# Tiles of float32r operands placed at multiples of 128 bytes in their partition

## The chip, the core and the metric

The kernel runs on one core of a Trainium2 chip. The metric is the device time of one execution in microseconds, as a median over several runs. The work of the core is done by TensorE (PE for its matmuls, PEld for the loads of its stationary operand), VectorE (DVE), ScalarE (ACT), GpSimd (POOL) and the DMA queue of SyncE (SP).

## The reference

Two blocks of two layers each run one after the other on 256 rows of width 1,024, all in float32. The first is a conditioned mixer with attention, gated linear attention and convolution, over 256 rows of context and 256 rows of x, each layer followed by a gated feed-forward part:

```
def _ffn(h, p):
    return (jax.nn.silu(h @ p['w_ff_gate']) * (h @ p['w_ff_up'])) @ p['w_ff_down']
```

The second block has a mixer of three kinds of attention and a feed-forward part with a short convolution:

```
for l in range(DEPTH):
    h = rms_norm(x, attn_pre_norm[l])
    mix = hybrid_mixer(h, cos, sin, w_in[l], ..., w_out[l])
    x = x + rms_norm(mix, attn_post_norm[l])
    h = rms_norm(x, ffn_pre_norm[l])
    x = x + rms_norm(conv_ffn(h, w_up[l], conv_w[l], conv_b[l], w_down[l]), ffn_post_norm[l])
```

Nearly all arithmetic is in products of 256 rows with weight matrices: `w_in`, `w_out` and the three feed-forward matrices of each layer.

## The kernel before

A float32 product is made of three float32r products. `split` and `weights` cut each operand into a rounded part `hi` and a remainder `lo`, both float32r, and `mm3` (lines 218 to 222) adds hi·hi, hi·lo and lo·hi in PSUM. In `gemm_f` the weights are the stationary operand, 128 columns at a time, and 256 rows of the input stream through them (512 where two streams share a weight). In `gemm_t` the input is stationary, and up to 512 columns of the weights stream. In a profile's name such as `g<-b,hi` the moving operand stands first.

Weights come by DMA on SP's queue into `raw` (`load`), ACT copies them to `hi` (line 210), and DVE subtracts to `lo` (line 213). The order of instructions on each engine is the Tile framework's, from a simulated timeline and the priorities that the code sets (`later`, `slot`).

Tiles live in pools: `wts` (raw, hi, lo), `cst` (constants), `sml` (small statistics), `com` (the inputs' hi and lo, tag `b16`, and rows), then `first` for the first block, and inside it, in turn, `mix0`, `ff`, `mix1` and `fx`. In the second block, `sec0` takes the place of `first`. Pools and tiles lie one behind the other in each partition, after a scratch of 16 KB for DMA descriptors and four constants. `Core.tile` gives every tile of a pool the size that its shape has, rounded to 32 bytes.

The position of a float32r operand in its partition, taken modulo 128 bytes, is here called its remainder. In the built program `wts` begins at 16,512 (remainder 0) and its tiles are 4,096 bytes each. `cst` begins at 53,376 and holds two tiles `cb2` of 32 bytes each; through these, `com` begins at 61,248 (remainder 64). `first` begins at remainder 64, and a tile of 8 bytes in it, `one`, puts all that follows at 96. `mix0`, `mix1`, `ff` and `fx` lie at 96, and the operands of `sec0` at 32. The 14,136 float32r products of the program stand at these remainders:

| columns that stream | remainder of moving | remainder of stationary | products |
|---|---|---|---|
| 256 | 64 (`com`) | 0 (`wts`) | 8,320 |
| 256 | 64 (`com`, `first`) | 96 (`first`, `ff`, `mix0`, `mix1`) | 992 |
| 256 | 0 (`wts`) | 64 (`com`) | 368 |
| 256 | 96 | 64 | 80 |
| 512 | 0 (`wts`) | 64 (`com`) | 1,584 |
| 512 | 64 (`com`) | 0 (`wts`) | 912 |
| 512 | 0 (`wts`) | 96 (`ff`, `fx`) | 680 |
| 512 | 0 (`wts`) | 32 (`sec0`) | 456 |
| 512 | 32 or 96 | 64 (`com`) | 240 |
| 512 | 96 (`mix`, `ff`, `fx`) | 96 | 112 |
| 512 | 32 (`sec0`) | 32 (`sec0`) | 72 |
| 284, 192 or 2 | various | various | 320 |

The other matmuls of the program are transposes and products in float32 and a few in bfloat16; a product in plain float32 stands in the trace as two matmuls.

Of the kernel before, what the change touches and what calls it, by code (L numbers as in the profile page):

```python
# [9 lines left out]
F32 = mybir.dt.float32  # L10
F32R = mybir.dt.float32r
BF16 = mybir.dt.bfloat16
I32 = mybir.dt.int32
U8 = mybir.dt.uint8
# [11 lines left out]
def together(**groups):  # L26
# [22 lines left out]
    'pg': dict(g=4),  # L49
    'pt': dict(t=4),  # L50
}


class Layout:
# [111 lines left out]
class Core:  # L166
# [4 lines left out]
    def tile(self, pool, shape, dt=F32, tag=None, bufs=None):  # L171

        self.n += 1
        kind = pool.name.rstrip('0123456789')
        tag = SHARE.get(kind, {}).get(tag, tag)
        n = bufs or BUFS[kind].get(tag, 1)
        return pool.tile(list(shape), dt, name=f"{tag}_{self.n}", tag=tag, bufs=n)

    @contextmanager
    def later(self, n):  # L180
# [136 lines left out]
class Second(Core):  # L317
# [177 lines left out]
    def rope(self, pr, h0, n):  # L495
        nc = self.nc
        for t in range(2):
            x = pr[t][:, h0 * 64:(h0 + n) * 64].rearrange("p (h d) -> p h d", d=64)
            x1, x2 = x[:, :, 0:8], x[:, :, 8:16]
            cos = self.cs2[:, 0, t][:, None, :].to_broadcast([128, n, 8])  # L500
            sin = self.cs2[:, 1, t][:, None, :].to_broadcast([128, n, 8])
            a, b, c, d = [self.tile(self.P, [128, 14, 8], F32, 'rp')[:, :n] for _ in range(4)]
            nc.vector.tensor_mul(a, x1, cos)
            nc.vector.tensor_mul(b, x2, sin)
            nc.vector.tensor_mul(c, x2, cos)
            nc.vector.tensor_mul(d, x1, sin)
            nc.vector.tensor_sub(x1, a, b)
            nc.vector.tensor_add(x2, c, d)
# [203 lines left out]
    def attend(self, proj, pr, v, rb, src):  # L712

        nc = self.nc
        proj(5)

        ga = self.tile(self.P, [128, 2, 8, 3], F32, 'ga')
        lf, e, z = [self.tile(self.P, [128, 2, 4], F32, 'lf') for _ in range(3)]
        for t in range(2):
            nc.vector.tensor_add(z[:, t], pr[t][:, P2['ff']:P2['ff'] + 4], rb[:, 0:4])  # L720
            nc.vector.tensor_add(ga[:, t].rearrange("p h j -> p (h j)"), pr[t][:, P2['ng']:P2['ng'] + 24], rb[:, 4:28])
        nc.scalar.activation(ga, ga, AF.Tanh, scale=0.5)
        nc.vector.tensor_scalar(ga, ga, 0.5, 0.5, op0=ALU.mult, op1=ALU.add)
        nc.scalar.activation(e, z, AF.Abs)
        nc.scalar.activation(e, e, AF.Exp, scale=-1.0)
        nc.scalar.activation(e, e, AF.Ln, bias=1.0)
        nc.vector.scalar_tensor_tensor(lf, z, 0.0, e, op0=ALU.min, op1=ALU.subtract)
        proj(1)
        pc = self.tile(self.PT, [128, 512], F32, 't')[:4, :256]
        nc.tensor.matmul(pc[:, :128], lf[:, 0], self.c('tri'), start=True, stop=True)  # L730
        nc.tensor.matmul(pc[:, 128:], lf[:, 0], self.c('ones'), start=True, stop=False)
        nc.tensor.matmul(pc[:, 128:], lf[:, 1], self.c('tri'), start=False, stop=True)
        crow = self.tile(self.P, [128, 256], F32, 's1')[:4]
        nc.vector.tensor_scalar(crow, pc, -1.0, None, op0=ALU.mult)
        proj(2)


        qk = {}

        def heads(*which):  # L740
            ps = self.tile(self.PT, [128, 2, 256], F32, 't')
            for j, (n, i) in enumerate(which):
                col = P2[n] + 128 * i
                for t in range(2):
                    nc.tensor.transpose(ps[:, j, t * 128:t * 128 + 128], pr[t][:, col:col + 128], self.ident)
            o = self.tile(self.P, [128, 2, 256], F32, 'qk')
            f = 0.125 if which[0][0][1] == 'q' else 1.0
            if len(qk) % 4:
                nc.scalar.activation(o, ps, AF.Copy, scale=f)
            else:  # L750
                nc.vector.tensor_scalar(o, ps, f, None, op0=ALU.mult)
            for j, key in enumerate(which):
                qk[key] = o[:, j]
        self.rope(pr, 8, 14)
        heads(('dq', 0), ('dq', 1))
        heads(('dk', 0), ('dk', 1))
        heads(('ks', 0), ('kw', 0))
        hi, lo = self.pair()
        PT_, cmp, queue = {}, {}, []

        def units(*gens, depth=DEPTH):
            for u in gens:
                next(u)
                queue.append(u)
                while len(queue) > depth:
                    next(queue.pop(0), None)
        scores = lambda t, w: self.nsa_scores(t, w, ('ks', 'kw')[w], w + 1, pr, qk, ga, PT_)
        four = lambda kind, base, t: self.heads4(kind, base, t, pr, qk, crow, hi, lo)
        units(four('d', 0, 0), four('d', 0, 1))
        ck = self.compress('k', pr, v, src, cmp)  # L770
        next(ck)
        proj(0)
        self.rope(pr, 0, 8)
        heads(('nq', 0), ('nq', 1))
        heads(('nq', 2), ('nq', 3))
        units(scores(0, 0))
        proj(3)
        next(ck, None)
        units(scores(0, 1))
        heads(('fq', 0), ('fq', 1))  # L780
        heads(('fk', 0), ('fk', 1))
        proj(4)
        cv = self.compress('v', pr, v, src, cmp)
        next(cv)
        units(four('f', 2, 0))
        next(cv, None)
        units(four('f', 2, 1), scores(1, 0), self.nsa_compressed(0, qk, cmp, ga, PT_),
              self.nsa_out(0, pr, cmp, PT_, hi, lo), scores(1, 1), self.nsa_compressed(1, qk, cmp, ga, PT_),
              self.nsa_out(1, pr, cmp, PT_, hi, lo))
        units(depth=0)  # L790
        while queue:
            next(queue.pop(0), None)
        return hi, lo
# [88 lines left out]
class First(Core):  # L882
# [589 lines left out]
    def mixer(self, L, s, X, full=True, src=None, rope=None, hook=None, hT=None, late=None):  # L1472
# [5 lines left out]
        if late:  # L1478
            late[0]()
            late.pop()()  # L1480
        glu = lambda j: self.gemm_f2(L.src('glu', j), hX)
        tabs = self.tables(L, rope)
        if full:
            ys = []
# [202 lines left out]
def build(tc, I, out):  # L1687
    nc = tc.nc
    K = Kernel(tc)
    rows = lambda a: [a[t * 128:t * 128 + 128] for t in range(2)]  # L1690
    left = lambda ends: dict(enumerate(ends))
    with ExitStack() as es:
        pool = lambda e, name, space=None: e.enter_context(tc.tile_pool(name=name, bufs=1, **({'space': space} if space else {})))
# [15 lines left out]
        for l in range(2):  # L1709
            L = Layer1(l, I[f'w1{l}'], LAYOUT[0][l], I[f'row1{l}'])  # L1710
            L.a2 = I[f'a2{l}']
            L.vec = K.tile(K.C, [128, I[f'vec1{l}'].shape[1]], F32, 'vec1')
            nc.sync.dma_start(L.vec, I[f'vec1{l}'])
            L.cb2 = K.tile(K.C, [128, 8], F32, 'cb2')
            nc.vector.tensor_scalar(L.cb2, L.v('cb', 8), 2.0, None, op0=ALU.mult)
            Ls.append(L)
        with ExitStack() as e1:
# [4 lines left out]
            first = K.rest[:2]  # L1722
# [68 lines left out]
```

## Time and profile before

| | us |
|---|---|
| median of 3 runs | 2732.79 |
| lowest and highest run | 2726.75, 2738.06 |
| the profiled execution: its own time | 2729.63 |
| the profiled execution: span from first to last instruction | 2727.8 |
| TensorE busy with matmuls | 2621.6 |
| VectorE busy | 1954.7 |
| ScalarE busy | 1383.3 |
| GpSimd busy | 137.8 |

A busy time is the union of the spans of an engine's instructions. TensorE's matmuls overlap: a new one starts while the results of the one before still drain, so the duration of one (276 ns and more) is longer than the step from one start to the next (113 ns and more). This step is called the pace here. It is read from the starts in the timeline, or from the number of matmuls in a stretch in which PE never rests: the stretch and one duration together, divided by the number, since a matmul is counted that only reaches into the stretch.

### The profile page before, as it was taken

What the parts mean: (1) busy time and instruction counts of PE and PEld (TensorE: products, weight loads), DVE (VectorE), ACT (ScalarE), POOL (GpSimd) and SP (SyncE); (2) the same over time, 40 slices, a digit from 0 to 9 for tenths busy, and PEclk for the clock granted to TensorE, in tenths of its full rate; (3) what the DMA queues carried; (4) which work ended last, traced back from release to release, by engine and by line L of the source; (5) the groups of instructions that cost most, each with busy time, mean ns of one, the idle gap of its engine ahead of it and who ended that gap; (6) DMA issues with size and microseconds to landing.
All of it is one profiled execution on the core that took longest, in us unless ns stands there. A gap on an engine that the chain in (4) does not pass through costs nothing.

```text
span 2727.8 us, 45641 instructions
## 1 busy us (share of the span) xinstructions
PE 2621.6 (96%) x17408; PEld 2271.2 (83%) x17408; DVE 1954.7 (72%) x3942; ACT 1383.3 (51%) x2524; POOL 137.8 (5%) x280
## 2 busy tenths in 40 slices
PE   7999999999999999999999999989989999999999
PEld 5977999977989888887797898979976699776997
DVE  4988977899967633355688997666676689556895
ACT  3555555545555422234754654544454566544663
POOL 0010011000001100001100100010010000000000
PEclk8999999999999999999999999989999999999999
DMA  7566456565535422222455433545554355542454
GB/s 255 187 224 206 163 178 211 185 208 180 179 116 206 173 93 93 93 93 100 154 167 201 160 120 117 172 152 186 186 183 148 110 170 196 172 160 93 163 193 155
DMA packets 127915, 443.34 MB, mean 163 GB/s; under 512 B 14888, under 2 KB 19112, under 8 KB 127696
## 3 DMA queue, kind: packets, MB, share of 16 engines
q1 hardware_dynamic: 127696, 440.43, 47.8%
q8 instruction: 137, 2.24, 0.3%
q14 instruction: 82, 0.67, 0.1%
HBM read 435.09 MB, written 5.28 MB: 161 GB/s over the span
## 4 chain that ended last, share of the span: by engine, by line
PE 88%; DVE 3%; DMA 3%; ACT 3%; issue 1%; POOL 1%; SPq 0%; DVEq 0%; POOLq 0%; ACTq 0%
PE g L221 21%; PE g L220 21%; PE g L222 20%; PE t L220 3%; PE t L222 3%; PE t L221 3%; DMA raw<-in_w_dram 3%; PE g L925 2%; PE t L1175 1%; PE t L1149 1%; PE t L1277 1%; PE t L1262 1%; PE t L1112 1%; PE t L1184 1%; PE g L663 1%
## 5 line engine op out<-in xcount | busy, mean ns | idle before, releaser
L213 DVE TENSOR_TENSOR lo<-raw,hi 128x512 fp32r<-128x512 f32 (+2 forms) x1280 | 824.8, 684 | 358.0 <-issue 157.3
L210 ACT CAST hi<-raw 128x1024 fp32r<-128x1024 f32 (+2 forms) x644 | 672.4, 1046 | 731.3 <-PE g L221 256.6
L220 PE MATMUL g<-b,hi 128*128 128x256 f32 (+1 forms) x2912 | 833.5, 288 | 4.4 <-ACT hi L210 3.9
L221 PE MATMUL g<-b,hi 128*128 128x256 f32 (+1 forms) x2912 | 829.4, 286 | 2.6 <-DVE b L311 2.5
L222 PE MATMUL g<-b,lo 128*128 128x256 f32 (+1 forms) x2912 | 823.4, 288 | 1.1 <-DVE lo L213 1.1
L220 PEld LDWEIGHTS g<-b,hi 128*128 128x128 f32 x2912 | 548.9, 189 | 15.1 <-ACT hi L210 4.3
L221 PEld LDWEIGHTS g<-b,hi 128*128 128x128 f32 x2912 | 549.4, 189 | 12.0 <-DVE b L311 3.9
L222 PEld LDWEIGHTS g<-b,lo 128*128 128x128 f32 x2912 | 542.1, 188 | 10.3 <-DVE lo L213 1.9
L1289 DVE SCALAR_TENSOR_TENSOR yc<-yc,vec,yc 128x256 f32<-128x256 f32 x720 | 345.4, 480 | 10.8
L221 PE MATMUL g<-lo,b 128*128 128x512 f32 (+2 forms) x712 | 271.4, 382 | 2.0 <-DVE lo L213 2.0
L222 PE MATMUL g<-hi,b 128*128 128x512 f32 (+2 forms) x712 | 264.7, 372 | 0.5 <-DVE b L314 0.4
L220 PE MATMUL g<-hi,b 128*128 128x512 f32 (+2 forms) x712 | 254.1, 377 | 11.2 <-ACT hi L210 5.7
L220 PEld LDWEIGHTS g<-hi,b 128*128 128x128 f32 x712 | 133.8, 191 | 38.5 <-ACT hi L210 6.5
L221 PEld LDWEIGHTS g<-lo,b 128*128 128x128 f32 x712 | 135.7, 191 | 30.7 <-DVE lo L213 6.2
L222 PEld LDWEIGHTS g<-hi,b 128*128 128x128 f32 x712 | 135.5, 190 | 22.2 <-DVE b L314 1.1
L220 PE MATMUL t<-b,hi 128*128 128x256 f32 (+1 forms) x336 | 112.6, 335 | 0.0
L221 PE MATMUL t<-b,hi 128*128 128x256 f32 (+1 forms) x336 | 112.6, 335 | 0.0
L222 PE MATMUL t<-b,lo 128*128 128x256 f32 (+1 forms) x336 | 112.4, 335 | 0.0
L477 DVE SCALAR_TENSOR_TENSOR s<-g,vec,s 128x255 f32<-128x255 f32 (+1 forms) x176 | 84.0, 478 | 6.0 <-ACT s L475 3.9
L925 PE MATMUL g<-raw,cs 128*32 128x256 f32 x768 | 67.7, 432 | 19.0 <-DMA raw<-in_w_dram 18.8
L221 PEld LDWEIGHTS t<-b,hi 128*128 128x128 f32 x336 | 63.7, 190 | 7.3
L220 PEld LDWEIGHTS t<-b,hi 128*128 128x128 f32 x336 | 63.2, 188 | 7.4
(421 smaller groups left out, 3928.7 us busy)
## 6 DMA issues: line engine op xcount, KB each, us to landing
raw<-in_w_dram SPq DMA_DIRECT2D x772, 512.0 KB, 3.8
b<-in_row_dram SPq DMA_DIRECT2D x16, 512.0 KB
b<-in_ctx_dram SPq DMA_DIRECT2D x4, 512.0 KB
ends<-st SPq DMA_DIRECT2D x8, 256.0 KB
st<-ends SPq DMA_DIRECT2D x8, 256.0 KB
b<-in_x_dram SPq DMA_DIRECT2D x4, 512.0 KB, 5.5
b<-ctx SPq DMA_DIRECT2D x4, 512.0 KB
raw<-in_w_dram SPq DMA_DIRECT2D x4, 426.0 KB
```

Of the source, the lines that this page charges most:

```text
L210: self.nc.scalar.copy(hi[:, :m], p)
L213: self.nc.vector.tensor_sub(lo[:, q], p[:, q], hi[:, q].bitcast(F32))
L220: t.matmul(ps, a[0], b[0], start=first, stop=False)
L221: t.matmul(ps, a[0], b[1], start=False, stop=False)
L222: t.matmul(ps, a[1], b[0], start=False, stop=last)
L477: nc.vector.scalar_tensor_tensor(c[:, m, j:], ps[:, m, :256 - j], cw[:, ft, 2 - j:3 - j], c[:, m, j:], op0=ALU.mult, op1=ALU.add)
L663: nc.tensor.matmul(ps[:, b], qk['nq', a * per + b][s, t * 128:t * 128 + 128], qk[kn, 0][s, :nk], start=False, stop=b == per - 1)
L925: m = nc.tensor.matmul(ps[32 * q:32 * q + 32, n * 256:n * 256 + 256], self.cs[:, h * 4 + q], raw[:, q * 256:q * 256 + 256], start=h == 0, ...
L1112: nc.tensor.matmul(p[:, h], kw[:, d, h * 128:h * 128 + 128], vg[:, h * 256:h * 256 + 256], start=True, stop=True)
L1149: nc.tensor.matmul(o, w, self.U[d][:, b * 256:b * 256 + n], start=d + i == 0, stop=d + i == 2)
L1175: nc.tensor.matmul(ps[:, a, h], G[h][b][:, a] if b < 3 else kT[:, h, ts], G[h][b][:, 2 + a], start=True, stop=True)
L1289: e.scalar_tensor_tensor(o, y[:, j:j + 256], w[:, j:j + 1], o, op0=ALU.mult, op1=ALU.add)
```

## The change

Every tile of two dimensions in the pools `first`, `mix0`, `mix1`, `ff`, `fx` and `sec0` is allocated with its row rounded up to 128 bytes, and used in its old size. Four kinds of small tiles with more dimensions are written as two-dimensional ones, so that they fall under this. The two tiles `cb2` in `cst` become 64 bytes long instead of 32, which moves `sml` and `com` behind them by 64 bytes. The scratch for DMA descriptors shrinks from 16,384 to 4,096 bytes, which moves everything down by 12,288 bytes (96 times 128).

```diff
+ALIGN = 128
+ALIGNED = ('first', 'mix', 'ff', 'fx', 'sec')
...
         n = bufs or BUFS[kind].get(tag, 1)
-        return pool.tile(list(shape), dt, name=f"{tag}_{self.n}", tag=tag, bufs=n)
+        make = lambda s: pool.tile(s, dt, name=f"{tag}_{self.n}", tag=tag, bufs=n)
+        size = {F32: 4, F32R: 4, I32: 4, BF16: 2, U8: 1}[dt]
+        if kind in ALIGNED and len(shape) == 2 and shape[1] * size % ALIGN:
+            step = ALIGN // size
+            return make([shape[0], -(-shape[1] // step) * step])[:, :shape[1]]
+        return make(list(shape))
...
-            a, b, c, d = [self.tile(self.P, [128, 14, 8], F32, 'rp')[:, :n] for _ in range(4)]
+            a, b, c, d = [self.tile(self.P, [128, 112], F32, 'rp').rearrange("p (h n) -> p h n", n=8)[:, :n] for _ in range(4)]
...
-        ga = self.tile(self.P, [128, 2, 8, 3], F32, 'ga')
-        lf, e, z = [self.tile(self.P, [128, 2, 4], F32, 'lf') for _ in range(3)]
+        ga = self.tile(self.P, [128, 48], F32, 'ga').rearrange("p (t h n) -> p t h n", h=8, n=3)
+        lf, e, z = [self.tile(self.P, [128, 8], F32, 'lf').rearrange("p (t h) -> p t h", h=4) for _ in range(3)]
...
-            L.cb2 = K.tile(K.C, [128, 8], F32, 'cb2')
+            L.cb2 = K.tile(K.C, [128, 16], F32, 'cb2')[:, :8]
...
-    nc = bacc.Bacc("TRN2", target_bir_lowering=False, num_devices=1)
+    nc = bacc.Bacc("TRN2", target_bir_lowering=False, num_devices=1, dynamic_dma_scratch_size=4096)
```

In the program built from it, `wts` begins at 4,224, `com` at 49,024, `first` and `sec0` at 114,560 and the others at 141,184: all have remainder 0. So both operands of every float32r product have remainder 0, except that the slices of 284 columns inside a weight tile still step by 1,136 bytes. The operands of `cst` stay where they were modulo 128. The list of instructions of each of the five engines is the same as before, in the same order and with the same waits; only addresses (and line numbers of the source) differ.

## Rows read from the trace of the kernel before

**Rows 1.** The page, parts 1 and 4: busy time of the engines, chain that ended last.

```profile
PE 2621.6 (96%) x17408; PEld 2271.2 (83%) x17408; DVE 1954.7 (72%) x3942; ACT 1383.3 (51%) x2524; POOL 137.8 (5%) x280
...
PE 88%; DVE 3%; DMA 3%; ACT 3%; issue 1%; POOL 1%; SPq 0%; DVEq 0%; POOLq 0%; ACTq 0%
```

**Rows 2.** Busy time, number, granted clock and DMA by stretch, all engines.

```profile
core 0: us, PE busy (x) PEld busy (x) DVE busy (x) ACT busy (x) POOL busy (x), PEclk, DMA share, GB/s
450.00:640.00 190.00, 187.29 (x1340) 164.24 (x1339) 171.54 (x363) 100.95 (x210) 17.38 (x24) 1.00 0.57 195
950.00:1164.00 214.00, 214.00 (x923) 171.71 (x922) 76.13 (x116) 51.71 (x60) 0.00 (x0) 1.00 0.27 91
2186.00:2303.00 117.00, 117.00 (x1030) 116.96 (x1029) 106.99 (x197) 75.12 (x105) 0.00 (x0) 1.00 0.55 186
2366.00:2541.00 175.00, 160.56 (x870) 119.12 (x870) 110.47 (x287) 90.61 (x221) 5.74 (x14) 0.94 0.37 127
```

**Rows 3.** The same view, PE alone, five stretches without rest.

```profile
2190.00:2300.00 110.00, 110.00 (x974) 1.00 0.57 193
1828.00:1938.00 110.00, 110.00 (x932) 1.00 0.56 187
960.00:1160.00 200.00, 200.00 (x859) 1.00 0.27 94
1165.00:1270.00 105.00, 105.00 (x449) 1.00 0.28 97
2310.00:2355.00 45.00, 45.00 (x195) 1.00 0.56 190
```

**Rows 4.** Timeline of PE, 34 matmuls: start, us, engine, line, op, out<-in, shapes, number.

```profile
2357.68 0.39 PE L220 MATMUL g<-h,h 128*128 128x512 f32 x1
...
2365.18 0.39 PE L220 MATMUL g<-h,h 128*128 128x512 f32 x1
```

**Rows 5.** Timeline of PE, 59 matmuls from first to last row.

```profile
885.81 0.39 PE L221 MATMUL g<-lo,b 128*128 128x512 f32 x1
...
899.09 0.39 PE L222 MATMUL g<-hi,b 128*128 128x512 f32 x1
```

**Rows 6.** Timeline of PE, 57 matmuls from first to last row.

```profile
943.80 0.28 PE L222 MATMUL t<-b,z 128*128 128x256 f32 x1
...
950.52 0.28 PE L220 MATMUL g<-b,z 128*128 128x256 f32 x1
```

**Rows 7.** Timeline of PE, 46 matmuls from first to last row.

```profile
194.81 0.28 PE L221 MATMUL g<-lo,b 128*128 128x256 f32 x1
...
200.00 0.28 PE L220 MATMUL g<-hi,b 128*128 128x256 f32 x1
```

**Rows 8.** Line 222: duration of one, ns (least/median/most), first and last start.

```profile
L222 PE MATMUL g<-b,lo x2912: 276/276/562, 41.2 to 2659.9; 128*128 128x256 f32 x182, 128*128 128x512 f32 x9, 128*32 128x256 f32 x4
...
L222 PE MATMUL t<-hi,z x88: 392/398/400, 1165.1 to 1225.3; 128*128 128x512 f32 x88
```

**Rows 9.** Timeline of PE, matmuls that stream two columns.

```profile
109.60 0.25 PE L1100 MATMUL t<-one,lgh 128*128 128x2 f32 x1
109.72 0.25 PE L1100 MATMUL t<-one,lgl 128*128 128x2 f32 x1
109.83 0.48 PE L221 MATMUL g<-lo,b 128*128 128x512 f32 x1
```

**Rows 10.** Chain of waits: sixteen matmuls of plain float32, 256 columns each.

```profile
125.08 3.45 PE t L1112 x16
```

**Rows 11.** Line 213 on DVE, by tile: duration of one, ns (least/median/most).

```profile
L213 DVE TENSOR_TENSOR lo<-raw,hi x1280: 417/684/715, 40.3 to 2708.6; 128x512 fp32r<-128x512 f32 x180, 128x256 fp32r<-128x256 f32 x2, 128x340 fp32r<-128x340 f32 x1
...
L213 DVE TENSOR_TENSOR h<-raw,h x28: 680/684/694, 2159.7 to 2711.2; 128x512 fp32r<-128x512 f32 x28
L213 DVE TENSOR_TENSOR gp<-raw,gp x12: 680/683/694, 454.4 to 1792.5; 128x512 fp32r<-128x512 f32 x12
```

**Rows 12.** The page, part 3: DMA queues, packets, MB, share of 16 engines.

```profile
q1 hardware_dynamic: 127696, 440.43, 47.8%
q8 instruction: 137, 2.24, 0.3%
q14 instruction: 82, 0.67, 0.1%
```

## The prediction

> **What bounds the kernel now.** I read the page's busy times and chain first, then the stretches, then single matmuls. PE is busy for 96% of the span and holds 88% of the chain that ended last [rows 1]; the reader is to see that no other engine comes near this over the whole span. By stretch the picture is less even: from 450 to 640 us DVE is busy for 171.54 of 190 us, from 2186 to 2303 us for 106.99 of 117, and from 2366 to 2541 us PE rests for some 14 us and has a granted clock of 0.94 [rows 2]. So a saving on PE counts nearly in full in the feed-forward stretches and with a discount elsewhere.
>
> The change moves addresses and nothing else: each engine's instructions stand in the same order with the same waits. So the question is only whether the address of an operand changes the time of an instruction. On PE the trace answers this in part, since the kernel before already holds equal products at different remainders. The pace says it:
>
> - 256 columns, moving 64, stationary 0: (110 + 0.28) / 974 = 113.2 ns, and in a mixed stretch, mostly of the same kind with some stationary operands at 96, (110 + 0.28) / 932 = 118.3 ns [rows 3].
> - 256 columns, moving 64, stationary 96: (950.52 - 943.80) / 56 = 120.0 ns [rows 6]. Moving 0, stationary 64: (200.00 - 194.81) / 45 = 115.3 ns [rows 7].
> - 512 columns, moving 64, stationary 0: (200 + 0.39) / 859 = 233.3 ns; moving 0, stationary 96: (105 + 0.39) / 449 = 234.7; moving 0, stationary 32: (45 + 0.39) / 195 = 232.8 [rows 3]. Moving 0, stationary 64: (899.09 - 885.81) / 58 = 229.0 [rows 5].
> - 512 columns, both at 32: (2365.18 - 2357.68) / 33 = 227.3 ns [rows 4].
>
> All of these run at a granted clock of 1.00, the 2.4 GHz level, at which 512 columns take 213.3 ns and 256 take 106.7. PE does not wait in them for data; it streams more slowly than its clock. The lowest pace among the 512-column products is that of equal remainders, and the pairs that differ by 32 or 96 are the slowest. Matmuls of plain float32, which spend two cycles on a column, show nothing of this: 16 of 256 columns take 3.45 us, 215.6 ns each against 213.3 [rows 10]. So the loss belongs to operands that are read at the full rate, and it hangs on where the two stand to each other.
>
> **The change part by part.** Remainder 0 on both sides is a pair that the trace of before doesn't show. The nearest row is the equal pair at 32, so I take 227.3 ns for 512 columns, and for 256 columns the fast pace of the present, 113.3, since the float32r stream of [rows 4] loses 14 ns on 512 columns and this one loses 6.6 on 256, the same loss per column. The terms, against the counts in the table of remainders:
>
> 1. 8,320 products of 256 columns, moving 64, stationary 0. The median of such a matmul is its least value, 276 ns [rows 8], so over half already run at the fast pace; the starts of the 8,156 of them under full clock, from 41.2 to 2659.8 us, give a mean pace of 115.1. To 113.3: 1.8 x 8,320 = 15.0 us.
> 2. 1,072 with a remainder of 96 on one side, between 118.3 and 120.0, say 118.5: 5.2 x 1,072 = 5.6 us. 368 with 0 and 64: 2.0 x 368 = 0.7 us.
> 3. 512 columns: 912 x (233.3 - 227.3) = 5.5 us; 680 x (234.7 - 227.3) = 5.0; 456 x (232.8 - 227.3) = 2.5; 1,584 x (229.0 - 227.3) = 2.7; 240 with 32 or 96 against 64, at about the 6 ns of the other unequal pairs, 1.4. Together 17.1 us.
>
> The sum is 38.4 us of PE's time. Of it I count 0.9, between the share of PE in the chain (0.88) and 1, as the largest terms lie where PE never rests: 35 us.
>
> At nothing I count the other edits. On DVE the subtraction `lo<-raw,hi` on tiles at 0 has a median of 684 ns, and the same on tiles at 96 (`gp`) or 32 (`h`) 683 and 684 [rows 11], so DVE gains and loses nothing by position; ACT's copies have the same operands, and I take the same for them. If that were wrong by 1% on DVE, most of it would be hidden by PE except in the two stretches named above, some 3 us. The smaller scratch costs nothing: all data move on the hardware queue, 127,696 packets, and only instruction fetches on others [rows 12]. The loads from memory keep their sizes and their tiles' remainder of 0.
>
> From above the gain is bounded by the full clock rate. A row of plain float32 shows an overhead of 2.3 ns over the cycles of a matmul [rows 10], so 512 columns could fall to 215.6. With 256 columns the load of the next stationary operand sets a floor: matmuls of two columns, which are nothing but such loads, follow each other after 0.12 and 0.11 us [rows 9], so there is hardly 2 ns below 113.3 to be had. From below: the pair 0 and 0 could be as bad as the worst rows, 120.0 and 234.7.
>
> [...]
>
> **The rivals.**
>
> *Only part counts.* Perhaps the 64-byte position is what matters, so that 0 and 64 are already as good as they get. Then the first term and the pairs of 0 and 64 stay, and 5.6 + 5.0 + 2.5 + 1.4 = 14.5 us remain, 13 on the path: 2720. For it: the largest group shows the fast pace for over a hundred microseconds at a time as it is. Against it: 233.3 for 64 and 0 with 512 columns, as slow as 0 and 32. Where nothing counts at all, or waits take up the gain, the time is 2733.
>
> *The stream gets free.* With both sides at the start of a 128-byte piece, the loss per column goes as well: 4,056 products of 512 columns from a mean of about 231 to 215.6 are 62 us, and 9,760 of 256 from 115.6 to 112 another 35; 0.9 of 97 is 87 us: 2646. For it: the half-rate rows have no loss. Against it: a moving operand at 0 is there already, with 229 at best.
>
> *Slower: both sides meet in the same place.* The two streams of a product would start in the same position of a 128-byte piece every time, and each load of a stationary operand would hold the moving stream up. If 256-column products went to the 120.0 of [rows 6], 8,320 x 4.9 = 41 us, and 1,584 of 512 columns from 229.0 to 234.7, 9 us, the kernel would take some 50 us longer: 2783. It decides from a pace of about 118 for 256 columns on. For it: the pair doesn't occur before with 256 columns, where a load fills the whole matmul. Against it: the equal pair at 32 is the fastest of all with 512, and the first half of such a matmul has the same load beside it.
>
> **How the numbers follow.** The profiled execution took 2729.63 us (span 2727.8), 3.2 below the median of 2732.79. Against the median the forecast is 2732.8 - 35 = 2697 us. Chances: this forecast 0.50 (2685 to 2712), only part or nothing 0.24 (2715 to 2735), the free stream 0.12 (2640 to 2665), slower 0.14 (2745 to 2790). The range from 2650 to 2738 leaves out the slower case and half of the free stream, 0.2. Within 0.5%, about what a measurement of this kernel can tell from no change, means 2719 to 2746. Faster are the forecast, the free stream and a small part of the second case: 0.65. The same: 0.22. Slower: 0.13. What could blur this by some microseconds either way are the stretches of lower clock, as from 2366 to 2541 us [rows 2], whose places shift when PE's rests shift.
>
> **What would show each step.** The terms show in the pace: stretches of 256 columns at 113 throughout, also where 118.3 stood, and 512 columns at 227 in all three feed-forward stretches of [rows 3]. DVE's 684 ns must stay [rows 11]. If PE's pace falls as said but the span doesn't, the gain went into waits for `hi` and `lo`, most likely between 450 and 640 us. A pace above 118 in the stretch from 2190 to 2300 us would make the forecast wrong in its sign; 216 with 512 columns would make it too small.

## The result and the profile after

| | before | after |
|---|---|---|
| median of 6 runs, us | 2733.51 (2726.75 to 2738.06) | 2757.80 (2755.44 to 2765.91) |
| profiled execution, us | 2729.63 | 2757.18 |
| its span, us | 2727.8 | 2755.2 |
| mean granted clock of the span | 0.981 | 0.975 |

The ratio is 1.0095, with a 95% interval of 1.0078 to 1.0113: the change costs 24 us, where the forecast was a gain of 35.

The page of the profile after, parts 1 and 4 (busy time of the engines; the chain that ended last):

```profile
PE 2652.1 (96%) x17408; PEld 2314.7 (84%) x17408; DVE 1957.2 (71%) x3942; ACT 1385.3 (50%) x2524; POOL 140.0 (5%) x280
...
PE 88%; DVE 3%; DMA 3%; ACT 3%; issue 1%; POOL 1%; SPq 0%; DVEq 0%; POOLq 0%; ACTq 0%
```

Against [rows 1], PE is busy for 30.5 us longer with the same 17,408 matmuls, and its share of the chain is the same 88%. The chain has no new member. DVE and ACT are busy for 2 to 3 us more. The subtraction, now on line 223, after (line, engine, operation, count: duration in ns, least/median/most):

```profile
L223 DVE TENSOR_TENSOR lo<-raw,hi x1280: 418/685/700, 41.6 to 2736.2; 128x512 fp32r<-128x512 f32 x180, 128x256 fp32r<-128x256 f32 x2, 128x340 fp32r<-128x340 f32 x1
...
L223 DVE TENSOR_TENSOR h<-raw,h x28: 682/685/694, 2175.6 to 2739.1; 128x512 fp32r<-128x512 f32 x28
L223 DVE TENSOR_TENSOR gp<-raw,gp x12: 684/689/693, 461.7 to 1806.3; 128x512 fp32r<-128x512 f32 x12
```

Most of `lo<-raw,hi` had remainder 0 before as well, so its 685 ns against the 684 of [rows 11] says little of position. The tiles that moved say it: `h`, from 32 to 0, took 684 and takes 685, and the twelve `gp`, from 96 to 0, took 683 and take 689, less than 1% more. So the loss lies in the pace of PE's matmuls. Stretches in the view of PE's rows, after (from:to in us, length, busy time and number of matmuls, granted clock, DMA share, GB/s): three of 256 columns, then three of 512.

```profile
2563.90:2686.40 122.50, 122.50 (x1022) 1.00 0.53 177
2202.10:2324.80 122.70, 122.70 (x1023) 1.00 0.53 177
1837.00:1956.70 119.70, 119.70 (x1000) 1.00 0.54 178
969.10:1295.00 325.90, 325.90 (x1440) 1.00 0.28 94
2327.40:2386.40 59.00, 59.00 (x263) 1.00 0.59 197
1165.00:1270.00 105.00, 105.00 (x465) 1.00 0.28 97
```

By the same working as in the prediction, 256 columns now take (122.7 + 0.28) / 1023 = 120.2 ns, and from start to start exactly 120.0 over the whole stretch. The part of this stretch in [rows 3] ran at 113.2. 512 columns take (325.9 + 0.39) / 1440 = 226.6 ns, where [rows 3] have 232.8 to 234.7.

Since both programs hold the same matmuls in the same order, each can be set beside itself. The time from the end of one matmul to the end of the next, summed by kind (remainders of moving and stationary before, modulo 128):

| products, full clock and no wait in either execution | before, us | after, us | difference |
|---|---|---|---|
| 256 columns, 64 and 0: 8,063 | 929.4 | 966.1 | +36.6 |
| 256 columns, 0 and 64: 347 | 40.5 | 41.5 | +1.0 |
| 256 columns, 64 and 96: 913 | 108.7 | 109.3 | +0.6 |
| 512 columns, 64 and 0: 912 | 212.8 | 206.7 | -6.1 |
| 512 columns, 0 and 96: 678 | 158.7 | 153.7 | -5.0 |
| 512 columns, 0 and 32: 454 | 105.9 | 103.0 | -2.9 |
| 512 columns, 0 and 64: 1,442 | 331.5 | 329.5 | -2.0 |
| 512 columns, the other unequal pairs and 96/96: 328 | 76.1 | 75.0 | -1.1 |
| matmuls in a stretch at the lower clock in one of the two | 132.9 | 138.6 | +5.6 |
| all the rest: waits, plain float32, narrow products | 578.4 | 578.1 | -0.3 |

The sum over all matmuls, with small groups that are left out here, is +26.3 us. One group carries it.

### The profile page after: what moved, and what is told of

It is laid out like the page before. It is cut to its first block, busy times and chain, and to the rows that moved or that the text cites. A ratio compares the mean times of both kernels' runs of the same rounds, so it can differ in the third digit from the quotient of the medians.

```text
span 2755.2 us, 45641 instructions
## 1 busy us (share of the span) xinstructions
PE 2652.1 (96%) x17408; PEld 2314.7 (84%) x17408; DVE 1957.2 (71%) x3942; ACT 1385.3 (50%) x2524; POOL 140.0 (5%) x280
## 4 chain that ended last, share of the span: by engine, by line
PE 88%; DMA 3%; DVE 3%; ACT 3%; issue 1%; POOL 1%; SPq 0%; DVEq 0%; POOLq 0%; ACTq 0%
PE g L231 21%; PE g L230 21%; PE g L232 21%; DMA raw<-in_w_dram 3%; PE t L231 3%; PE t L230 3%; PE t L232 3%; PE g L935 2%; PE t L1159 1%; PE t L1185 1%; PE t L1287 1%; PE t L1272 1%; PE t L1122 1%; PE t L1194 1%; PE t L1284 1%
## 5 line engine op out<-in xcount | busy, mean ns | idle before, releaser
L230 PE MATMUL g<-b,hi 128*128 128x256 f32 (+1 forms) x2912 | 845.0, 292 | 2.6 <-ACT hi L220 2.0
L231 PE MATMUL g<-b,hi 128*128 128x256 f32 (+1 forms) x2912 | 841.5, 290 | 2.4 <-DVE b L321 2.2
L232 PE MATMUL g<-b,lo 128*128 128x256 f32 (+1 forms) x2912 | 834.4, 292 | 1.1 <-DVE lo L223 1.1
L230 PEld LDWEIGHTS g<-b,hi 128*128 128x128 f32 x2912 | 556.5, 191 | 12.2 <-ACT hi L220 2.5
L231 PEld LDWEIGHTS g<-b,hi 128*128 128x128 f32 x2912 | 556.6, 191 | 10.8 <-DVE b L321 3.7
L232 PEld LDWEIGHTS g<-b,lo 128*128 128x128 f32 x2912 | 550.1, 191 | 9.2 <-DVE lo L223 1.9
L230 PEld LDWEIGHTS t<-b,hi 128*128 128x128 f32 x336 | 64.0, 190 | 6.3
L232 PEld LDWEIGHTS t<-b,lo 128*128 128x128 f32 x336 | 63.8, 190 | 6.3
```

Source lines behind the costliest of these rows:

```text
L230: t.matmul(ps, a[0], b[0], start=first, stop=False)
L231: t.matmul(ps, a[0], b[1], start=False, stop=False)
L232: t.matmul(ps, a[1], b[0], start=False, stop=last)
```

## The experiments

The theory that the result suggests: the pace of a float32r product is set by where its two operands lie to each other, and the equal pair, which is the best for 512 columns, is the worst for 256 (theory P; it counts remainders modulo 128, as the change does). Its first rival is that the other part of the change, the smaller scratch, which also shifts every tile by 12 KB, costs the time.

### The scratch alone, and the remainder of `com` alone

The kernel before with 12 KB taken from the scratch, and nothing else:

```
-    nc = bacc.Bacc("TRN2", target_bir_lowering=False, num_devices=1)
+    nc = bacc.Bacc("TRN2", target_bir_lowering=False, num_devices=1, dynamic_dma_scratch_size=4096)
```

> The kernel before with the smaller scratch for DMA descriptors alone: everything moves down by 12,288 bytes, all remainders stay. Theory P: 2733 us, the same paces as before (113.3 in the stretch of 256 columns near 2200 us, 233.3 near 1000 us). Rival S (the scratch, or bits of the address above 128 bytes, cost the 24 us): 2745 to 2760 us.

Measured: 2734.19 us, ratio 1.0008 (0.9995 to 1.0021). The scratch and the shift cost at most 0.2%, and the rival asked for 0.4% or more.

The changed kernel with `com` back at 64, everything else at 0:

```
-            L.cb2 = K.tile(K.C, [128, 16], F32, 'cb2')[:, :8]
+            L.cb2 = K.tile(K.C, [128, 8], F32, 'cb2')
...
+            K.tile(K.B, [128, 2, 8], F32, 'pad')
...
+            K.tile(K.P, [128, 2, 8], F32, 'pad')
```

> The changed kernel with the pool com put back to remainder 64 and all other pools kept at 0 (cb2 of 32 bytes again, and a tile of 64 bytes ahead in first and in sec0). Theory P: the 8,320 products of 256 columns have 64 and 0 again, pace 115 on average instead of 120, 37 us less than the changed kernel; the products of 512 columns with com lose their gain again (0 and 64, 64 and 0: 8 us more), those with ff, fx and sec0 keep it (8 us). 2722 to 2728 us, so 0.2 to 0.4% faster than before. Rival S or A (small tiles, scratch or the absolute position of the other pools make it slow): 2745 to 2760 us.

Measured: 2721.20 us, ratio 0.9955 (0.9938 to 0.9971), 1 us below what theory P expects. And the kernel before with `com` alone at 0; the two pads keep the pools behind it at their old remainders, and the smaller scratch is in it too:

```
-            L.cb2 = K.tile(K.C, [128, 8], F32, 'cb2')
+            L.cb2 = K.tile(K.C, [128, 16], F32, 'cb2')[:, :8]
...
+            K.tile(K.B, [128, 2, 8], F32, 'pad')
...
+            K.tile(K.P, [128, 2, 8], F32, 'pad')
...
-    nc = bacc.Bacc("TRN2", target_bir_lowering=False, num_devices=1)
+    nc = bacc.Bacc("TRN2", target_bir_lowering=False, num_devices=1, dynamic_dma_scratch_size=4096)
```

> The kernel before with the pool com alone put to remainder 0 (cb2 of 64 bytes, smaller scratch, and a tile of 64 bytes ahead in first and in sec0, which leaves those and the pools behind them at their old remainders). Theory P: the 8,320 products of 256 columns go to 120.0 ns, 37 us more; the 1,584 and 912 of 512 columns to 226.7 ns, 8 us less; ff, fx and sec0 as before. 2757 to 2765 us, slower than the changed kernel itself by some 5 us. Rival S or A: 2733 us, since the rounded small tiles are not in it.

Measured: 2759.69 us, ratio 1.0101 (1.0087 to 1.0114), as theory P expects. The two kernels in the last long stretch of 256 columns, PE's rows; first with `com` at 64, then with `com` at 0:

```profile
2538.00:2648.00 110.00, 110.00 (x973) 1.00 0.55 192
```

```profile
2566.00:2682.00 116.00, 116.00 (x969) 1.00 0.53 184
```

113.3 against 120.0 ns, by 64 bytes in the address of the moving operand. These 64 bytes make the kernel before as slow as the changed one, and taking them back makes the changed one faster than both: the rest of the change is a gain.

### Matrix engine alone: is it the addresses?

In the kernel other engines read and write the same memory all the time [rows 1]. The next kernel has none of that: 192 float32r products for each pair of positions, four repetitions of 48, each after a lead, which is one product of another length (128, 2, 320 or 200 columns).

```
+    out = [(n, m, s) for n in (256, 512) for m in 'abcd' for s in 'abcd']
+    return out + [(256, 'a', s) for s in 'efghi'] + [(256, m, 'a') for m in 'efghi']
```

> This kernel leaves the reference's work out: it copies x to the output and runs only float32r matmuls from two large tiles, 192 in a row for each pair of remainders (moving, stationary) modulo 128 bytes, with 256 and 512 columns; PSUM tiles are named by the pair (a 0, b 32, c 64, d 96, e 16, f 48, g 80, h 112, i 4; s for 256 columns, l for 512). No other engine works beside it. Theory P (the pair of remainders alone sets the pace): 256 columns with equal remainders 120.0 ns; moving 64 and stationary 0 113.3 or 117.8; moving 0 and stationary 64 113 to 118; 64 and 96 120. 512 columns with equal remainders 226.7 ns; 64 and 0 233.3; 0 and 64 229; 0 and 32 233; 0 and 96 234. Rival C (the loss comes from traffic of other engines and DMAs into the same memory, which the alignment only shifts): all pairs of one size alike here, near 108 to 113 and 216 to 227 ns. Rival A (the absolute position counts, not the difference): all pairs with moving 0 alike, whatever the stationary operand's remainder.

PE's rows, in windows from the second to the last start of one repetition, so that each holds 46 paces: 256 columns, both operands at 32; moving 0 and stationary 64, in two repetitions; then 512 columns, both at 0; moving 0 and stationary 64:

```profile
142.53:148.05 5.52, 5.52 (x48) 1.00 0.01 3
73.21:78.62 5.41, 5.41 (x48) 1.00 0.00 0
78.97:84.20 5.23, 5.23 (x49) 1.00 0.00 0
408.45:418.88 10.43, 10.43 (x47) 1.00 0.01 2
498.42:509.15 10.73, 10.73 (x47) 1.00 0.01 2
```

So 5.52 / 46 = 120.0 ns for the equal pair with 256 columns. All pairs, in ns from product to product once the pace of a repetition has settled (0, 32, 64 and 96 are remainders modulo 128; two values are two repetitions of the same pair):

| | 256 columns | 512 columns |
|---|---|---|
| equal pair, all four | 120.0 | 226.7 |
| moving 0, stationary 64 | 113.3 or 117.8 | 233.3 |
| moving 64, stationary 0 | 117.8 | 228.8 (once 233.3) |
| moving 0, stationary 96 | 117 to 120 | 234.3 |
| moving 0, stationary 32 | 118.4 | 233.3 |
| moving 96, stationary 0 | 120.0 | 233.3 |

Equal pairs at 0, 32, 64 and 96 agree, so the absolute position is not what counts, and with the other engines at rest the pace is the same, so it is not their traffic. One thing was odd: moving 0 and stationary 64 behaved like the kernel's "64 and 0", and the other way round. On this theory P's values for 64 and 0 with 512 columns, and for 0 and 64, came out swapped, and 64 and 96 with 256 columns gave 118.3 and not 120.

### Finer steps, narrower loads, other lengths

From here on each pair has six repetitions of 30 products, after leads of 128, 2, 320, 200, 256 and 512 columns. A case is (columns that stream, position of moving, position of stationary, columns of stationary):

```
...
+    out = [(256, 0, s, 128) for s in range(8, 128, 4) if s not in (16, 32, 48, 80, 96, 112)]
+    out += [(n, 0, s, c) for n in (256, 512) for s in (0, 64) for c in (64, 32)]
+    return out + [(n, 0, 0, 128) for n in (384, 320, 192, 128)]
```

> This kernel leaves the reference's work out, as the one for the pairs did: it copies x to the output and runs float32r matmuls alone, 180 in a row for each case. It varies three things: the remainder in steps of 4 bytes with 256 columns (tiles named by remainder / 32 as a to d and remainder in it / 4 as a to h, moving first), the width of the stationary operand (128 columns: n, 64: h, 32: q), and the number of columns that stream (128 to 384 with equal remainders). Theory L (the moving stream runs into the load of the next stationary operand; its own rate costs one cycle in seventeen): with 64 and 32 stationary columns at equal remainders the pace falls from 120.0 towards 113.3 for 256 columns, about 116.7 with 64 columns, and 512 stays at 226.7; 113.3 with a moving operand at 112 and a stationary one at 0 in every repetition. Rival W (the loss above the full clock rate is all from weight loads): with 32 stationary columns 256 go to 108 to 109 ns and 512 to 216. Rival D (the difference of the remainders alone counts): 0 and 16, 16 and 32, 48 and 64, 112 and 0 all alike.

Measured with an equal pair: 256 columns go from 120.0 to 113.5 ns when the stationary operand has 64 columns in place of 128; with 32 they settle at 113.3 in four repetitions and at 117.8 in two. 512 columns go the other way, from 226.7 to 229.9 and 231.5. So the 120.0 hangs on the width of the stationary operand, but a narrow one does not free the stream: rival W's 108 and 216 did not come. Theory L missed as well: it wanted about 116.7 with 64 stationary columns, an unchanged 226.7, and 113.3 in every repetition for moving 112 and stationary 0, which gave 113.3 to 115.9.

The other lengths of an equal pair say what its loss is. PE's rows with 384, 320, 192 and 128 columns; the first window holds 27 paces, the others 28:

```profile
1151.32:1156.00 4.68, 4.68 (x29) 1.00 0.02 4
1170.93:1175.04 4.11, 4.11 (x31) 1.00 0.00 0
1199.46:1202.59 3.13, 3.13 (x30) 1.00 0.00 0
1209.94:1213.07 3.13, 3.13 (x30) 1.00 0.00 0
```

From the starts, once the pace has settled:

| columns, both at 0 | pace, ns | columns x 0.4167 ns | loss, ns |
|---|---|---|---|
| 512 | 226.67 | 213.33 | 13.3 |
| 384 | 173.33 | 160.00 | 13.3 |
| 320 | 146.66 | 133.33 | 13.3 |
| 256 | 120.0 | 106.67 | 13.3 |
| 192 | 111.65 | 80.00 | 31.7 |
| 128 | 111.67 | 53.33 | 58.3 |

The third column is what the lengths from 256 to 512 show: (226.67 - 120.0) / 256 = 0.4167 ns for each further column, 2.4 columns in a ns. The trace of before has the same rate at a granted clock of 0.50, where float32r products of 512 columns follow each other after 427 ns, twice the 213.3 that the prediction set beside its paces (start, duration, engine, line, operation, shapes, number):

```profile
1319.85 0.63 PE L222 MATMUL g<-hi,b 128*128 128x512 f32 x1
1320.28 0.63 PE L220 MATMUL g<-hi,b 128*128 128x512 f32 x1
1320.70 0.63 PE L221 MATMUL g<-lo,b 128*128 128x512 f32 x1
1321.13 0.63 PE L222 MATMUL g<-hi,b 128*128 128x512 f32 x1
```

The last two of the table are as long as the step of the two-column matmuls in [rows 9], 0.12 and 0.11 us, beside which the loads of the stationary operand start every 0.11 us (PEld in the trace of before: 109.58, 109.69, 109.80 us). The others lose the same 13.3 ns, as much as 32 columns take, whatever their length: an equal pair pays by the matmul and not by the column. As each matmul has one load (17,408 of each in the kernel's page), the runs can't tell whether it is the load that costs it. With the stationary operand moved in steps of 4 bytes the 256-column pace jumped between 113.3 and 122.3 with no plain order, and with moving at 104 and stationary at 0 three repetitions reached 130.0. At one offset, 76, all six repetitions stood at 113.3 to 113.7. A moving operand at 112 with the stationary one at 112 gave 118.3 (256 columns) and 231.1 (512), so at positions that are no multiple of 32 the difference is not all that counts.

### A place for each role of a weight

The changed kernel, with `com` at 64 and weight tiles of 4,224 bytes, in `wts` used from byte 64 for products of 512 columns and from byte 0 for those of 256 (the other way round in `first`, whose base lies at 64). `eq` is true for weights of 512-column products:

```
...
+        at = 16 if (pool is self.W) == eq else 0
+        return self.tile(pool, [128, 1056], F32R, tag)[:, at:at + 1024]
...
```

> The changed kernel with the remainder chosen by kind of product: com, first, mix, ff, fx and sec0 at 64, and the hi and lo tiles of wts one row of 128 bytes longer, used from byte 64 where 512 columns stream (both operands at 64) and from byte 0 where 256 do (64 and 0, as before). Theory P: 256 columns at 115 on average and 120 for the 592 of unequal or equal kinds in ff and mix, 512 columns at 226.7 throughout: 17 us less than before on those of 512 columns and some 3 us on the 512 products whose stationary tile lies in first: 2711 to 2718 us, 5 to 10 us below the version with com alone put back. Rival S or A: 2730 us or more.

Measured: 2721.89 us, ratio 0.9971 (0.9955 to 0.9987), less than expected. The 256 columns ran at 114.6 as wanted, but 512 columns with 64 on both sides took 230.2 and not 226.7. Among those that stand between neighbours of their own kind they split in two: 1,318 products at a mean of 228.0, whose addresses differ by a multiple of 256, and 650 at 232.8, whose addresses differ by 128 more. The tiles of 4,224 bytes, 33 times 128, had put every second tile 128 bytes off modulo 256. For 512 columns theory P counted modulo the wrong number.

The 256 columns had the same split, and there it made no difference. In the program of this kernel 622 of the 1,021 products of the stretch from 2,179 to 2,294 us have the stationary operand 192 bytes ahead of the moving one, modulo 256, and 399 have it 64 ahead; the three long stretches, PE's rows:

```profile
1821.00:1931.00 110.00, 110.00 (x973) 1.00 0.55 189
2180.00:2290.00 110.00, 110.00 (x973) 1.00 0.55 192
2534.00:2644.00 110.00, 110.00 (x973) 1.00 0.56 195
```

(110 + 0.28) / 973 = 113.3 ns throughout, so products 192 ahead can run at 113.3 as well.

### The period

```
+    out = [(256, 0, s, 128) for s in (0, 16, 32, 48, 52, 64, 72, 76, 80, 96, 112, 124, 128, 132, 136, 140, 144, 148, 152, 156, 160, 164, 168, 172, 176, 180,
+                                      184, 188, 192, 196, 200, 204, 208, 216, 224, 232, 240, 244, 248, 252, 256, 320, 332, 384, 400, 448)]
+    out += [(256, m, 0, 128) for m in (64, 76, 128, 192)] + [(256, 64, 140, 128), (256, 128, 128, 128)]
+    return out + [(512, 0, s, 128) for s in (0, 64, 128, 192, 256, 384)] + [(512, 128, 0, 128)]
```

> Only the matrix engine works here, on float32r products, 180 per pair of positions, with no part of the reference but the copy of x; each pair is a moving operand at one byte remainder and a stationary operand (128 columns) at another, and what counts is the pace inside a pair. The mixed kernel put 512-column products at remainder 64 on both sides, and they split by a thing that a remainder of 128 does not see: where the two addresses differ by a multiple of 256 bytes the pace was 228.04 ns (1,318 products, mostly 226 and 227), where they differ by 128 more it was 232.75 (650). Theory Q, the rule repeats every 256 bytes: with moving at 0, stationary at 128 and 384 gives about 233 with 512 columns and 118 with 256, stationary at 256 gives 226.7 and 120.0 as at 0, and stationary at 192 gives what moving 64 ahead of the stationary gave earlier (228.8 with 512 columns, 116 to 118 with 256), and not what stationary at 64 gives (233.3 and 113.3 or 117.8). Theory P, it repeats every 128 bytes: 128, 256 and 384 all give 226.7 and 120.0, and 192 gives 233.3 and 113.3 or 117.8. The rest of the offsets, in steps of 4 to 16 bytes, looks for a pair at which 256 columns hold 113.3 in all repetitions, as stationary at 76 did; by Q it should appear again at 332, by P also at 204.

PE's rows, in windows from the second to the last start of one repetition, so that each holds 28 paces; moving at 0, stationary at 0, 64, 76, 128, 256 and 332 with 256 columns, then at 0, 64, 128, 192 and 256 with 512:

```profile
23.04:26.40 3.36, 3.36 (x30) 1.00 0.02 5
...
131.22:134.52 3.30, 3.30 (x30) 1.00 0.00 0
...
174.89:178.06 3.17, 3.17 (x30) 1.00 0.00 0
285.56:288.87 3.31, 3.31 (x30) 1.00 0.00 0
905.35:908.71 3.36, 3.36 (x30) 1.00 0.00 0
952.55:955.73 3.18, 3.18 (x30) 1.00 0.00 0
1175.21:1181.57 6.35, 6.35 (x29) 1.00 0.00 0
1217.30:1223.83 6.53, 6.53 (x29) 1.00 0.01 3
1260.08:1266.61 6.53, 6.53 (x29) 1.00 0.00 0
1302.58:1308.99 6.42, 6.42 (x29) 1.00 0.01 3
1344.67:1351.03 6.35, 6.35 (x29) 1.00 0.00 0
```

3.36 / 28 = 120.0 ns at 0 and again at 256, but 3.31 / 28 = 118.2 at 128; 6.35 / 28 = 226.8 at 0 and 256, 6.53 / 28 = 233.2 at 64 and 128, 6.42 / 28 = 229.3 at 192. Theory Q holds for these: what lies 256 bytes apart behaves alike, 128 apart does not, and 76 comes back at 332 (and as 64 against 140), in all repetitions 113.3 to 113.7, but not at 204 (120.4).

With this the kernel before can be read. In its addresses modulo 256, `wts` lies at 128 and `com` at 64, so "64 and 0" is a stationary operand 64 ahead, and "0 and 64" one 192 ahead:

| stationary ahead by, modulo 256 | 256 columns, kernel before | 256, PE alone | 512 columns, kernel before | 512, PE alone |
|---|---|---|---|---|
| 0 | not there | 120.0 | 227.8 | 226.9 |
| 32 | 118.2 | 118.3 | 233.3 | 233.3 |
| 64 | 115.1 (113.3 and 117.8) | 113.3 or 117.8 | 233.3 | 233.3 |
| 96 | 118.8 (few) | 118.2 | 234.3 | 234.3 |
| 160 | 119.9 | 120.0 | 233.4 | 233.3 |
| 192 | 116.6 | 117.8 | 229.7 | 229.6 |

In the row of 192 PE alone gave 117.8 in every repetition, where the kernel with a place for each role held 113.3 for 1,000 products: with 256 columns the difference does not settle the pace by itself.

### Both lengths at their better difference

The changed kernel with weight tiles of 4,352 bytes (17 times 256). Weights of 512-column products start at byte 0 of the tile, so that the pair is equal; those of 256-column products start at byte 64, in the second kernel at byte 76 (19 in place of 16):

```
...
+    def placed(self, pool, tag, eq):
+        at = 0 if eq else 16
+        return self.tile(pool, [128, 1088], F32R, tag)[:, at:at + 1024]
...
```

> The changed kernel, with a second place for the weight pairs: those of 256-column products start 64 bytes into their tile (the tiles are 4,352 bytes long, a multiple of 256), those of 512-column products stay at its start. So 512-column products have both operands at one remainder of 256, and of the 256-column ones about 8,690 have the stationary operand 64 bytes behind the moving one's remainder, as in the kernel before. Theory Q (the pace follows the difference of the two addresses modulo 256): 512 columns 226.7 to 227.4 ns, 256 columns 114 to 115.1; against the kernel before the 512-column stretches give back 16 to 17 us, as in the changed kernel, and the 256-column ones nothing or up to 6 us: a ratio of 0.992 to 0.995, 2,709 to 2,717 us. If 256 is not the period that matters in the kernel, 512 columns stay mixed at about 230 as in the mixed kernel, and it comes out as that did, at 0.997, 2,722 us.

> The same with 76 bytes in place of 64: the 256-column products' stationary operand lies 76 bytes further, modulo 256, than their moving one, the one difference at which the matrix engine alone kept 113.33 ns in every repetition (0 and 76, 0 and 332, 64 and 140). Theory Q: 256 columns at 113.3 to 113.6, 512 columns at 226.7 to 227.4, so that some 8,690 products lose the second pace of 117.8 that a part of them has at 64 (mean 115.06 in the kernel before): 13 to 15 us less than the kernel with 64, a ratio to the kernel before of 0.986 to 0.990, 2,692 to 2,704 us. Rival R, the second pace comes from what the other engines do or from gaps between groups and not from the addresses: 256 columns stay a mixture near 114.5 to 115 and the time equals that of the kernel with 64, 0.992 to 0.995.

Measured: 2711.76 us with 64, ratio 0.9927 (0.9904 to 0.9951), as theory Q expects; 2705.16 us with 76, ratio 0.9907 (0.9886 to 0.9929), 1 us outside what it expects. (What the expectation with 64 calls behind is called ahead here.) Both beat the kernel before and the changed one; that 76 beats 64 is not shown, as the two intervals overlap. 512 columns have a mean of 227.3 in both. The long stretches of 256 columns, PE's rows, with 64 and then with 76:

```profile
1817.00:1927.00 110.00, 110.00 (x937) 1.00 0.57 187
2178.00:2288.00 110.00, 110.00 (x973) 1.00 0.57 193
2527.00:2642.00 115.00, 115.00 (x979) 1.00 0.55 185
```

```profile
1813.00:1919.00 106.00, 106.00 (x938) 1.00 0.59 194
2170.00:2280.00 110.00, 110.00 (x973) 1.00 0.57 192
2522.00:2638.00 116.00, 116.00 (x969) 1.00 0.54 183
```

The reader is to see that a stretch keeps one pace to its end: with 64, 117.7, 113.3 and 117.8 ns; with 76, 113.3 twice, then 120.0 for 1,019 products. So a difference of 76 has a second pace too, which did not appear with PE alone. Over all, the mean with 76 was 114.78, in the 114.5 to 115 of rival R and not in theory Q's 113.3 to 113.6; with 64 on the same chip it was 115.68, above the 114 to 115.1 that theory Q expects. Theory Q is right on 512 columns and on the equal pair, but the choice between the paces of 256 columns does not follow from the difference alone. How the last stretch with 76 begins (start, duration, engine, line, operation, shapes, number):

```profile
2518.66 0.40 PE L238 MATMUL g<-b,hi 128*128 128x256 f32 x1
2518.88 0.31 PE L239 MATMUL g<-b,lo 128*128 128x256 f32 x1
2519.02 0.28 PE L237 MATMUL g<-b,hi 128*128 128x256 f32 x1
2519.14 0.28 PE L238 MATMUL g<-b,hi 128*128 128x256 f32 x1
```

Its pace is 120 from the first product after the granted clock came back from the lower level to 1.00 (starts 0.21 or 0.22 us apart up to 2518.88, 0.12 from 2519.02 on; a clock of 0.50 shows 213 ns in the kernel before), and nothing later changes it. But the two stretches at 113.3 begin at such a return as well (1,809.0 and 2,167.4 us), so the return does not decide it. What would steer the entry was not tried.

## Why the prediction was wrong

**What bounds the kernel: right.** PE holds 88% of the chain as before, and the difference lies in PE's pace and, for 5.6 us, in its clock; waits and all other work changed by -0.3 us. DVE took 685 against 684 ns for the moved `h` and 689 against 683 for the moved `gp`, and the run with the scratch alone came out at 1.0008.

**That position sets the pace: right, counted by a wrong number.** The prediction sorted the pairs by their remainders modulo 128, as the change does. The period is 256 (at 76 and at 332 the pace was 113.3 to 113.7 ns, at 204 it was 120.4). By luck of the layout the changed kernel is equal modulo 256 nearly everywhere as well (of the 256-column products that follow one another at full clock 8,997, against 96 that are 128 off), so this cost the forecast nothing, but it hid why 64 and 0 and 0 and 64 differ. The prediction calls the pairs that are 32 or 96 apart the slowest of 512 columns, but its own lines have 64 and 0 at 233.3, above the 232.8 of 0 and 32. That nothing counts and the time stays at 2733, which the prediction allowed for, did not come: with PE alone the same product of 256 columns took 113.3 to 130.0 ns by the place of its operands.

**512 columns: right.** Term 3 was 17.1 us; the two traces give 6.1 + 5.0 + 2.9 + 2.0 + 1.1 = 17.1, and the pace is the 227 that was taken from [rows 4]. That the sums agree to 0.1 us is luck: the parts are off by up to 0.7 us either way.

**256 columns, term 1: this step failed.** It took 113.3 ns for the equal pair, on the ground that the equal pair at 32 with 512 columns loses the same per column as the fast pace with 256. The loss of an equal pair is not per column. It is the same 13.3 ns for every matmul from 256 to 512 columns, so the 14.0 ns of [rows 4] (227.3 against the 213.3 of 512 columns at 0.4167 ns), carried over by the matmul, would have given 106.7 + 14.0 = 120.7. The 113.3 belongs to another pair, a stationary operand 64 ahead, which loses 6.7 with 256 columns and 20 with 512. That 6.7 is about half of 14.0 was chance. So 8,063 products took 36.6 us more, where term 1 had 15.0 us less, and the sign of the whole turned. The rows spoke for both readings, as only one equal pair and one length were there; the prediction named the load beside the stream in the rival that ends slower, and then argued it away with the 512-column row.

**Term 2** has the same fault, in small: the pairs with 96 stood at 120 and stay there (+0.6 where -5.6 was forecast), and 0 and 64 went from 117 to 120 (+1.0 for -0.7).

**The rival "both sides meet in the same place"** had the right pair and its price for 256 columns (120.0 and 41 us; measured 36.6). Whether the load holds the stream up, as it says, is not shown: narrower loads brought 256 columns down to 113.5, but 512 columns up to 229.9. Its 2783 was too high because it let 512 columns grow worse too, by 9 us, where they gained 17. With 120.0 in terms 1 and 2 and term 3 left as it is, the prediction's own sum is 8,320 x 4.9 + 1,072 x 1.5 + 368 x 4.7 - 17.1 = 27 us, 2760. It was given 0.14, and the range was cut just above the kernel before, so that it left out the price that the prediction itself had set as the bound from below.

**The clock.** Matmuls in stretches at the lower of the two clocks, 0.50 against 1.00, in one execution or the other, make +5.6 us, as the prediction allowed for. One that moved with a rest of PE, as it said: the rest of 1.97 us that ends at 2368.0 us before and at 2389.0 after has a stretch at 0.50 behind it, from 2370.9 us on before and from 2390.0 us on after. All six runs of the changed kernel have a mean granted clock of 0.975 or 0.976, so it is not a matter of one execution. The slower stream of 256 columns does not bring it by itself: the kernel before with `com` alone at 0 has the same 120.0 ns and 0.979 to 0.980 in all four runs. What does is open.

## What to carry to other kernels

A loss that was measured at one length of the moving operand can be carried to another length by the column or by the matmul, and the two differ by a factor: work out both, and where no row with the same length decides, give the worse one a serious chance. Where a pattern by address looks uneven under one modulus (here 64 and 0 against 0 and 64), try twice the modulus before extrapolating. This kernel, bound by PE with float32r products, gained 0.7 to 0.9% by layout alone, with equal addresses modulo 256 for 512 columns and the stationary operand 64 or 76 bytes ahead for 256. In the two traces some 17 us of this lie in the 512 columns; the place for the 256 columns mainly avoids the 37 us of the equal pair.

## What the runs showed of the hardware

- The pace of a float32r product hangs on how far, modulo 256 bytes, the stationary operand lies ahead of the moving one: 226.7 to 234.3 ns with 512 columns, 113.3 to 130.0 with 256, at a granted clock of 1.00 and with no other engine at work. Among positions at multiples of 32 the equal pair is the best with 512 columns (226.7) and, level with 160 ahead, the worst with 256 (120.0). At other positions, as with both at 112, the difference does not give the pace.
- At a granted clock of 1.00 each further column of an equal pair from 256 to 512 columns takes 0.4167 ns. Such a pair costs 13.3 ns, as much as 32 columns, above its columns for each matmul from 256 to 512 columns, and a matmul of 128 or 192 columns takes 111.7 ns, as long as the step of the two-column matmuls in [rows 9].
- A run of 256-column products at some differences takes one of two paces when it begins and keeps it. With PE alone and the stationary operand 64 ahead, leads of 128, 200 and 256 columns gave 113.3, and leads of 2, 320 and 512 gave 117.8, the same with moving at 0 and stationary at 64 and at 320; with moving at 192 and stationary at 0, also 64 ahead, it was leads of 200, 256 and 320 that gave 113.3. In the kernel stretches of 1,000 products stayed at 113.33, 117.78 or 120.00 throughout. The same last stretch, with the same differences, ran at 113.3 in the kernel before and at 117.8 in the one with the smaller scratch, PE's rows of each:

```profile
2545.00:2655.00 110.00, 110.00 (x973) 1.00 0.58 194
```

```profile
2547.00:2661.00 114.00, 114.00 (x970) 1.00 0.54 187
```

So some microseconds of a difference between single executions, 4.3 for the 970 products here, can come from the pace that a stretch fell into.
- Why 256 bytes, why the steps of 4 bytes follow no plain order, and what picks the pace of a run, stays open.
